# Two-layer speech encoder on one core: a correction transfer issued apart from its cast, plain down projections in every last chunk, and the opening norm sums moved into the second pair

## The chip, the core and the metric

The kernel runs on one core of one Trainium2 chip. The metric is the device time in microseconds (us); lower is better. One execution was also taken by the hardware profiler, and its profile is what this document reads. The engines run side by side, each through its own list of instructions in order: TensorE (PE, with its weight loads as PEld), VectorE (DVE), ScalarE (ACT), GpSimd (POOL) and SyncE (SP), which issues most of the DMA transfers.

## The reference

Two layers work on 512 tokens of 1024 features, all in float32. Each layer is a half-step SwiGLU feed-forward, a mixing part (attention and a convolution side by side), a second half-step SwiGLU feed-forward, and a last norm:

```python
def swiglu(x, w_gate, w_up, w_down):
    return (jax.nn.silu(x @ w_gate) * (x @ w_up)) @ w_down
...
    for l in range(DEPTH):
        x = x + 0.5 * swiglu(rms_norm(x, ffn1_norm[l]), ffn1_w_gate[l], ffn1_w_up[l], ffn1_w_down[l])
        h = rms_norm(x, mix_norm[l])
        p = h @ w_in[l]
...
        x = x + jnp.concatenate([attn, conv], axis=-1) @ w_out[l]
        x = x + 0.5 * swiglu(rms_norm(x, ffn2_norm[l]), ffn2_w_gate[l], ffn2_w_up[l], ffn2_w_down[l])
        x = rms_norm(x, post_norm[l])
```

The hidden width of each feed-forward is 2816, that is 22 blocks of 128.

## The kernel before

**Layout.** The features of x lie on the 128 partitions in eight tiles x[:, m], the 512 tokens along the free dimension. A float32 product is made of three passes: each operand is split into a rounded part (hi, type fp32r) and the rest (lo), and `mm3` (lines 152 to 154) adds weight-hi by data-hi, weight-hi by data-lo and weight-lo by data-hi into a PSUM bank. Weights are split as they arrive: a DMA into a `raw` or `fr` tile, a cast on ACT (the hi part, `wh`), and a subtraction on DVE (the lo part, `wl`). `load_w` does so for a plain product (lines 134 to 142), `split_into` for a quarter or a sum of quarters (lines 251 and 253).

**Feed-forward.** `ffn` is called four times: ffn1 and ffn2 of both layers. Its 22 hidden blocks are worked off as 11 pairs p, in four chunks of pairs, (0,1), (2,3,4), (5,6,7) and (8,9,10). In the first chunk gate and up are plain products with 512 columns (`plain`), and the result is scaled by R, the inverse root of the norm sums, only behind the product (`plain_out`, lines 300 to 305). From pair 2 on, a pair is made by seven products of quarter matrices in place of eight (`pair`, the scheme of Strassen and Winograd): the weight is loaded in quarters a11, a12, a21, a22 (line 280), four sums of them are formed on DVE, and every product has 24 matmuls of 256 columns. The data operands of these products (b11, t1, t2 and so on) are made once from x and R by the steps of the generator `operands` (lines 313 to 355), which `advance` hands out between other work. The down projection of a chunk is likewise made by seven products for each half g of the output (`down`, lines 435 to 499; 18 matmuls of 256 columns each), and each product is added to x at line 462. In the last chunk this held for ffn1 of both layers; ffn2 of both layers already had the plain form there: eight groups m of 18 matmuls of 512 columns, added to x at line 554, each followed by `done(m)`, which makes the operand of the next stage from x[:, m] (lines 165 and 166) and adds its square to the norm sums (lines 191 to 198).

**Two of the seven products** (with a12, called b21, and with a22, called t4, the fourth product) get their lo part in another way, in `summed` (lines 372 to 380): ACT writes the negated rounded quarter into a tile `ls` (line 376), and a DMA issued by POOL adds the float32 quarter from memory to it (line 377). `ls` has two buffers. Then ACT casts hi (line 379). In `down` this whole step stood at the fourth product's own place, behind the casts of the products t2, t3 and t1.

**Tiles that come round.** `fr` has four buffers, `raw` three, `wh` and `wl` four each, and PSUM gives seven banks of 512 columns. A quarter goes to an `fr` tile, except a12 and the sum s3, which go to `raw`.

**Order.** The program is written in one order and a scheduler places each engine's instructions; `tc.issue_after(order[...])` and `after(...)` hold an instruction behind a named one. From then on each engine works in order, and waits at an instruction until what it needs is there.

**The opening.** In the first ffn of layer 0 the norm sums of x stand behind pair 0. Each x[:, m] is squared on ACT; the squares were added into two sums, one by DVE and one by POOL. Sixteen tiny matmuls (8 instructions, line 205) sum them over the features, DVE scales the result (line 212), POOL takes the root (line 171), DVE lays it on a diagonal (line 220), one float32 matmul spreads it (line 224) and ACT copies it out as R (line 230). All of this stood between pair 0 and pair 1 on PE:

```python
                    if w0:
                        norm()
                        R = norm()
                    steps = operands(R)
```

Of the kernel before, what the change touches and what calls it, by code (L numbers as in the profile page):

```python
# [15 lines left out]
P = 128  # L16
# [21 lines left out]
NC = 3  # L38
# [34 lines left out]
def encoder_kernel(ctx: ExitStack, tc: tile.TileContext, xT, consts, vecs, rgain, wgu1, wd1, wdq1,  # L73
# [99 lines left out]
    class Stats:  # L173
# [5 lines left out]
        def add(self, src, scale=1.0, last=False, eng=None, apart=False, second=False):  # L179
            if second and self.tail is not None:  # L180
                sq = tmp()
                A.activation(sq, src, AF.Square, scale=scale)
                eng.tensor_tensor(self.tail, self.tail, sq, ALU.add)
                return
            if second:
                self.tail = slot()
                A.activation(self.tail, src, AF.Square, scale=scale)
                return
# [11 lines left out]
        def sums(self):  # L200
            ps = bank()
            parts = [self.acc] + ([self.tail] if self.tail is not None else [])
            for part in parts:
                for t in range(NT):
                    T.matmul(ps[:, t:t + 1], part[:, t * P:(t + 1) * P], ones[:, 0:1],
                             start=part is self.acc and (t == 0 or len(parts) == 1), stop=part is parts[-1],
                             skip_group_check=len(parts) > 1)
# [31 lines left out]
    def groups(srcs, rhs, ws=None):  # L239
# [16 lines left out]
    def ffn(l, gx, norm, wgu, wd, wdq, gain, done, w0=None, halved=KD, straight=False):  # L256
        with tc.tile_pool(name="f", bufs=4) as fpool:
            ffn_body(fpool, l, gx, norm, wgu, wd, wdq, gain, done, w0, halved, straight)

    def ffn_body(fpool, l, gx, norm, wgu, wd, wdq, gain, done, w0, halved, straight):  # L260
# [15 lines left out]
        def quarters(w, n):  # L276

            a = quarter(), late(), quarter(), quarter()
# [93 lines left out]
        def summed(w, src, n=WC):  # L372

# [3 lines left out]
            G.dma_start(out=lo[:, :n], in_=w, accum_op=ALU.add)  # L377
            hi = wpool.tile([P, WC], FR, tag="wh", name=nm("wh"))
# [3 lines left out]
        def pair(p, quartered):  # L382

            a11, a12, a21, a22, s3 = quarters(wgu[l, p], WC)
# [50 lines left out]
        def down(act, chunk):  # L435

            n = 2 * NP * P

            def finish(m):

                if chunk == NC - 1:
                    with after("added"):
                        done(m)
                        done(m + 1)

            for g in range(2):
# [3 lines left out]
                def times(o, src, name, start, q=None):  # L450
# [753 lines left out]
```

## Time and profile before

| What | Value |
|---|---|
| Median of 3 runs | 1835.67 us (1835.55 to 1839.94) |
| Profiled execution, device time | 1838.1 us |
| Its span in the profile | 1836.3 us |
| Granted TensorE clock, mean | 0.992 of full speed |
| Memory read, written | 225.30 MB, 2.10 MB |
| DMA into `ls` for a down quarter (384 KB), issue to landing, median | 6.7 us, 40 of them |
| DMA into `fr` for a gate and up quarter (512 KB), median | 4.1 us, 108 of them |

The profiled execution is 2.4 us above the median, and what lies around the span is 1838.1 - 1836.3 = 1.8 us. In the rows that follow, an instruction is given as engine, line and operation, then what it writes and what it reads; `x3` behind it counts instructions that the row takes together. In square brackets stands the time for which the engine had been idle just before, and what ended that. A row of windows gives, for one stretch of time, its length, the busy time of the engine with its number of instructions, the granted TensorE clock as a share of full speed, the busy share of the DMA engines, and what they moved.

### The profile page before, as it was taken

How to read it: one execution, taken by the hardware profiler on the slowest of the kernel's cores; microseconds unless marked ns; L12 is line 12 of the kernel's file. 1: busy time of each engine (PE TensorE's matmuls, PEld its weight loads, DVE VectorE, ACT ScalarE, POOL GpSimd, SP SyncE). 2: the span in 40 equal slices, each digit the busy share in tenths (PEclk: the TensorE clock that was granted, in tenths of full speed). 3: DMA queues.
4: the chain of work that ended last, by engine and by line, in shares of the span. 5: the costliest groups of instructions: out<-in, count | busy, mean ns of one | idle time of the engine just before them, and what ended most of it. 6: DMA issues, size and time to landing. Idle time of an engine off the chain costs nothing. (4 is left out here: it accounts for less than half of the span.)

```text
span 1836.3 us, 31207 instructions
## 1 busy us (share of the span) xinstructions
PE 1793.5 (98%) x12422; PEld 1663.6 (91%) x12422; DVE 1464.7 (80%) x2039; ACT 1108.7 (60%) x1717; POOL 435.4 (24%) x354
## 2 busy tenths in 40 slices
PE   8999999999999999999999999998999999999998
PEld 7899999888788899999889999998888788999997
DVE  6888888879965978887679878787899568878874
ACT  4565656557954565656635656565679435656564
POOL 2001000238944000000310000103579410010101
PEclk9999999999999999999999999999999999999999
DMA  4555656423303456565326474744250125465642
GB/s 163 158 138 154 156 151 157 116 76 116 69 1 110 127 155 155 149 160 139 117 68 167 112 193 113 195 116 136 75 140 21 42 85 172 119 176 135 173 116 76
DMA packets 71570, 229.42 MB, mean 125 GB/s; under 512 B 8064, under 2 KB 8448, under 8 KB 71424
## 3 DMA queue, kind: packets, MB, share of 16 engines
q1 hardware_dynamic: 54000, 169.74, 27.9%
q0 software_dynamic: 17280, 57.68, 17.8%
q8 instruction: 97, 1.59, 0.3%
q14 instruction: 49, 0.40, 0.1%
q10 hardware_dynamic: 144, 0.00, 0.0%
HBM read 225.30 MB, written 2.10 MB: 124 GB/s over the span
## 5 line engine op out<-in xcount | busy, mean ns | idle before, releaser
L152 PE MATMUL ps<-r,wh 128*128 128x256 f32 (+1 forms) x3508 | 1075.4, 309 | 6.4 <-DVE x L462 5.2
L153 PE MATMUL ps<-r,wh 128*128 128x256 f32 (+1 forms) x3508 | 1076.4, 307 | 0.0
L154 PE MATMUL ps<-r,wl 128*128 128x256 f32 (+1 forms) x2692 | 844.0, 315 | 1.4 <-DVE wl L253 0.6
L152 PEld LDWEIGHTS ps<-r,wh 128*128 128x128 f32 x3508 | 669.1, 191 | 40.6 <-issue 6.8
L153 PEld LDWEIGHTS ps<-r,wh 128*128 128x128 f32 x3508 | 670.7, 191 | 33.1 <-issue 2.7
L154 PEld LDWEIGHTS ps<-r,wl 128*128 128x128 f32 x2692 | 514.4, 191 | 34.1 <-POOL wl L142 1.3
L154 PE MATMUL ps<-r,ls 128*128 128x256 f32 x816 | 232.8, 285 | 19.7 <-DMA ls<-in_wdq 18.6
L136 ACT CAST wh<-raw 128x1024 fp32r<-128x1024 f32 (+4 forms) x132 | 118.7, 908 | 199.9 <-PE ps L153 112.3
L377 POOL DMA_DIRECT2D ls<-in_wgu x72 | 62.8, 878 | 740.8 <-ACT ls L376 695.8
L251 ACT CAST wh<-fr 128x1024 fp32r<-128x1024 f32 (+1 forms) x168 | 163.3, 972 | 97.4 <-DVE fr L392 29.4
L253 DVE TENSOR_TENSOR wl<-fr,wh 128x1024 fp32r<-128x1024 f32 (+1 forms) x168 | 189.7, 1129 | 34.6 <-ACT wh L251 34.6
L142 DVE TENSOR_TENSOR wl<-raw,wh 128x1024 fp32r<-128x1024 f32 (+4 forms) x116 | 132.1, 1146 | 70.1 <-ACT wh L136 69.5
L154 PEld LDWEIGHTS ps<-r,ls 128*128 128x128 f32 x816 | 155.5, 191 | 22.0 <-DMA ls<-in_wdq 20.7
L892 POOL TENSOR_TENSOR y<-y,pr 128x511 f32<-128x511 f32 (+14 forms) x120 | 157.5, 1313 | 54.2 <-ACT pr L888 46.9
L253 DVE TENSOR_TENSOR wl<-raw,wh 128x1024 fp32r<-128x1024 f32 (+1 forms) x112 | 125.9, 1124 | 28.4 <-ACT wh L251 27.9
L251 ACT CAST wh<-raw 128x1024 fp32r<-128x1024 f32 (+1 forms) x112 | 108.8, 972 | 37.5 <-PE ps L153 21.7
L462 DVE SCALAR_TENSOR_TENSOR x<-ps,x 128x512 f32<-128x512 f32 x140 | 96.2, 687 | 38.7 <-PE ps L154 37.9
L377 POOL DMA_DIRECT2D ls<-in_wdq x40 | 34.6, 865 | 349.7 <-ACT ls L376 315.8
L198 POOL TENSOR_TENSOR r<-r,t 128x512 f32<-128x512 f32 x45 | 78.6, 1755 | 118.7 <-ACT t L194 108.5
L376 ACT ACTIVATE ls<-fr 128x1024 fp32r<-128x1024 f32 (+1 forms) x56 | 55.1, 984 | 82.3 <-PE ps L154 55.7
L888 ACT ACTIVATE pr<-r,vec 128x511 f32<-128x511 f32 (+14 forms) x120 | 85.2, 734 | 9.7 <-POOL y L892 9.7
L884 DVE SCALAR_TENSOR_TENSOR cv<-r,vec,cv 128x511 f32<-128x511 f32 (+14 forms) x120 | 87.6, 730 | 3.4 <-ACT cv L880 2.1
(222 smaller groups left out, 2486.9 us busy)
## 6 DMA issues: line engine op xcount, KB each, us to landing
fr<-in_wgu SPq DMA_DIRECT2D x108, 512.0 KB, 4.1
ls<-in_wgu POOLq DMA_DIRECT2D x72, 512.0 KB, 5.6
raw<-in_wgu SPq DMA_DIRECT2D x66, 512.0 KB, 4.7
fr<-in_wdq SPq DMA_DIRECT2D x60, 384.0 KB, 4.6
ls<-in_wdq POOLq DMA_DIRECT2D x40, 384.0 KB, 6.7
raw<-in_wd SPq DMA_DIRECT2D x32, 256.0 KB, 2.7
raw<-in_wcv SPq DMA_DIRECT2D x16, 512.0 KB, 3.7
raw<-in_wout SPq DMA_DIRECT2D x16, 512.0 KB, 3.3
```

Of the source, the lines that this page charges most:

```text
L136: order["cast"] = A.copy(hi[:, :w], raw[:, :w]).ins
L142: (G if kind in POOLW.split() else V).tensor_tensor(lo[:, :w], raw[:, :w], hi[:, :w].bitcast(FP), ALU.subtract)
L152: T.matmul(o, lh, rh, start=first, stop=False, skip_group_check=free)
L153: T.matmul(o, lh, rl, start=False, stop=False, skip_group_check=free)
L154: order["mm"] = T.matmul(o, ll, rh, start=False, stop=last, skip_group_check=free).ins
L251: A.copy(hi[:, :w], src[:, :w])
L253: order["lo"] = V.tensor_tensor(lo[:, :w], src[:, :w], hi[:, :w].bitcast(FP), ALU.subtract).ins
L377: G.dma_start(out=lo[:, :n], in_=w, accum_op=ALU.add)
L462: return V.scalar_tensor_tensor(v, o.rearrange("p (m t) -> p m t", m=2), 0.5 * sign, v, ALU.mult, ALU.add).ins
L884: V.scalar_tensor_tensor(acc[:, s:], u[c][:, :S - s], tap(k), acc[:, s:], ALU.mult, ALU.add)
L888: A.activation(pr[:, s:], u[c][:, :S - s], AF.Copy, scale=tap(k))
L892: order["conv"] = G.tensor_tensor(acc[:, s:], acc[:, s:], pr[:, s:], ALU.add).ins
```

## The change

Three places change. First, `summed` is cut in two: `subtracted` writes the negated cast and issues the transfer, and `down` calls it for the fourth product ahead of the casts of t3, t1 and t4 itself. Second, the last chunk of every ffn takes the plain down projection; `down` loses its calls of `done`, and the weights in quarters cover two chunks, not three. Third, the opening norm sums stand within pair 1 (the second pair): the sums behind half of its first product, the spread behind its second, and all squares are added by DVE into one sum. With it come two small edits: in pair 2 the quarter a12 goes to an `fr` tile, and in the mixing part the first two groups take seven blocks of features, not six, before the rest.

```diff
-NC = 3
+NC = 2
...
-                    T.matmul(ps[:, t:t + 1], part[:, t * P:(t + 1) * P], ones[:, 0:1],
...
+                    order["sums"] = T.matmul(ps[:, t:t + 1], part[:, t * P:(t + 1) * P], ones[:, 0:1],
...
-        for ks in (range(KD - 2), range(KD - 2, KD)):
+        for ks in (range(KD - 1), range(KD - 1, KD)):
...
-            a = quarter(), late(), quarter(), quarter()
+            a = quarter(), quarter() if first else late(), quarter(), quarter()
...
-        def summed(w, src, n=WC):
-
+        def subtracted(w, src, n=WC):
 
             lo = fpool.tile([P, WC], FR, tag="ls", name=nm("ls"), bufs=2)
             A.activation(lo[:, :n], src[:, :n], AF.Copy, scale=-1.0)
             G.dma_start(out=lo[:, :n], in_=w, accum_op=ALU.add)
+            return lo
+
+        def summed(w, src, n=WC, lo=None):
+
+            lo = subtracted(w, src, n) if lo is None else lo
             hi = wpool.tile([P, WC], FR, tag="wh", name=nm("wh"))
             A.copy(hi[:, :n], src[:, :n])
             return hi, lo
...
+                lo = subtracted(wdq[l, g, chunk, 3], a22, n)
                 with after("u"):
                     times(pz, s3, "t3", True)
                 add(1, 1, pz, 1)
                 with after("v"), after("vh"):
                     times(px, a21, "t1", False)
                     order["first"] = add(1, 1, px, -1)
-                    times(pz, a22, "t4", False, 3)
+                    times(pz, a22, "t4", False, 3, lo)
...
-            last = p1 == NF // 2 and (straight or halved < KD)
+            last = p1 == NF // 2
...
-                    if w0:
-                        norm()
-                        R = norm()
-                    steps = operands(R)
-                    for o in os:
-                        act.append(plain_out(o, R))
+                    if not w0:
+                        scaled(os, R)
...
-                        plain(o, ws, range(KD))
+                        if w0 and not r:
+                            with tc.issue_after(order["mm"]):
+                                plain(o[:1], ws, KS[:KD // 2])
+                            with tc.issue_after(order["mm"]):
+                                norm()
+                            with after("sums"):
+                                plain(o[:1], ws, KS[KD // 2:])
+                                plain([None] + o[1:], ws, range(KD))
+                            with tc.issue_after(order["mm"]):
+                                R = norm()
+                            scaled(os, R)
+                        else:
+                            plain(o, ws, range(KD))
...
-            second = KS.index(m) % 2 == 1
-            st.add(x[:, m, :], eng=G if second else V, second=second)
+            st.add(x[:, m, :], eng=V)
```

`scaled(os, R)` makes the generator `operands(R)` and calls `plain_out` on pair 0's two outputs. In the changed file lines 154 and below keep their numbers; the sums stand at line 196, the spread at 215, the copy of R at 221, and lines 376, 379, 410 and 251 become 366, 374, 405 and 242.

ACT in the down projection of the first quartered chunk of layer 0, first half g, before. `e` and `t` in the second row are the silu of the pair just ended; `ls_1624` is the fourth product's negated cast, `wh_1627` its hi cast:

```order
L369 COPY e_1346<-ps_1248 128x512
L410 ACTIVATE t_1438<-e_1346 128x512
L251 CAST wh_1554<-fr_1492 128x768
L159 CAST r_1474<-t_1438 128x512
L251 CAST wh_1578<-raw_1500 128x768
L413 ACTIVATE t_1315<-ps_1248 128x256
L159 CAST r_1484<-u_1478 128x512
L159 CAST r_1488<-t_1479 128x512
L251 CAST wh_1601<-fr_1494 128x768
L376 ACTIVATE ls_1624<-fr_1495 128x768
L379 CAST wh_1627<-fr_1495 128x768
```

The same place in the changed program:

```order
L360 COPY e_1343<-ps_1245 128x512
L366 ACTIVATE ls_1575<-fr_1492 128x768
L405 ACTIVATE t_1435<-e_1343 128x512
L242 CAST wh_1551<-fr_1489 128x768
L159 CAST r_1471<-t_1435 128x512
L242 CAST wh_1578<-raw_1497 128x768
L408 ACTIVATE t_1312<-ps_1245 128x256
L159 CAST r_1481<-u_1475 128x512
L366 ACTIVATE ls_1703<-raw_1669 128x768
L159 CAST r_1485<-t_1476 128x512
L242 CAST wh_1601<-fr_1491 128x768
L374 CAST wh_1624<-fr_1492 128x768
```

The fourth product's negated cast (now `ls_1575`) has moved up by eight instructions, ahead of the silu at the head of the list, and its transfer on POOL with it.

PE in the opening, before: the end of pair 0, the sums, the spread, and the first matmuls of pair 1:

```order
L154 MATMUL ps_253<-r_158,wl_175 128x512
L205 MATMUL ps_303<-ones,r_177 128x1 x4
L205 MATMUL ps_303<-ones,r_179 128x1 x4
L224 MATMUL ps_317<-t_315,ones 128x512
L152 MATMUL ps_355<-r_105,wh_345 128x512
```

And in the changed program, first at the sums, which 12 matmuls of pair 1 now precede, then at the spread, 36 matmuls further on:

```order
L154 MATMUL ps_315<-r_132,wl_307 128x512
L196 MATMUL ps_330<-ones,r_177 128x1 x4
L152 MATMUL ps_315<-r_143,wh_311 128x512
...
L153 MATMUL ps_316<-r_159,wh_311 128x512
L154 MATMUL ps_316<-r_158,wl_313 128x512
L215 MATMUL ps_376<-t_374,ones 128x512
L152 MATMUL ps_443<-r_105,wh_433 128x512
```

So half of pair 1's 96 matmuls stand ahead of the spread now, where all of them stood behind it.

PE a little later in the changed program, in the down projection of the first chunk, where the groups 0 to 3 (`ps_531`, `ps_553`, `ps_578`, `ps_604`) go over from the third operand (`r_427`, `r_428`) to the fourth, which comes from pair 1's second product (hi `r_527`, lo `r_528`):

```order
L154 MATMUL ps_604<-r_427,wl_609 128x512
L152 MATMUL ps_531<-r_527,wh_534 128x512
L152 MATMUL ps_553<-r_527,wh_556 128x512
L152 MATMUL ps_578<-r_527,wh_581 128x512
L152 MATMUL ps_604<-r_527,wh_607 128x512
L153 MATMUL ps_531<-r_528,wh_534 128x512
```

Ahead of this place stand 36 matmuls of the four groups, and behind it 60, as before; what has moved is what stands ahead of the 36: 48 matmuls behind the spread, where there were 96.

More of the change, by code (lines that the diff above doesn't have):

```diff
@@ L177, in __init__, with add @@
             self.acc = self.tail = None
[L179 to L188, printed above, removed]
+        def add(self, src, scale=1.0, last=False, eng=None, apart=False):
             if self.acc is None:
@@ L382, in pair @@
         def pair(p, quartered):
-            a11, a12, a21, a22, s3 = quarters(wgu[l, p], WC)
+            a11, a12, a21, a22, s3 = quarters(wgu[l, p], WC, p == CHUNKS[0][1])
             bx, by, bz = bank(), bank(), bank()
@@ L448, in down, with times @@
                 px, py, pz = bank(), bank(), bank()
[L450 to L451 removed]
+                def times(o, src, name, start, q=None, lo=None):
+                    hi, lo = split_into(name, src, n) if q is None else summed(wdq[l, g, chunk, q], src, n, lo)
                     with tc.issue_after(order["pe"]):
@@ L496, in down, with scaled @@
                 add(0, 1, px, 1)
-                if chunk == NC - 1 and g:
-                    done(6)
-                    done(7)
         steps = None
+        def scaled(os, R):
+            nonlocal steps
+            steps = operands(R)
+            for o in os:
+                act.append(plain_out(o, R))
         def advance(n):
```

35 lines of the change are left out of this document (11 added, 24 removed).

## The prediction

> **What bounds the kernel now.** I read the busy shares first, then what PE waited for, then the stages around those waits.
>
> ```profile
> PE 1793.5 (98%) x12422; PEld 1663.6 (91%) x12422; DVE 1464.7 (80%) x2039; ACT 1108.7 (60%) x1717; POOL 435.4 (24%) x354
> 170.00:240.00 70.00, 70.00 (x589) 1.00 0.57 143
> 890.00:925.00 35.00, 35.00 (x156) 1.00 0.34 117
> ```
>
> PE is busy for 98% of the span, so two things can change the time: the number and width of its matmuls, and the little time in which it stands or runs at a lower clock. The two windows give its pace at full clock. In a stretch of pairs it starts 589 matmuls of 256 columns in 70 us, 0.119 us each; in a plain down projection 156 of 512 columns in 35 us, 0.224 each. A plain column is thus slightly cheaper, and I use these paces, not the duration of one matmul, since matmuls overlap. Next, the list of PE's waits:
>
> ```profile
> PE ps L154 <- DMA ls<-in_wdq: 18.6, 10, 2.1
> PE ps L152 <- DVE x L462: 5.2, 2, 2.6
> PE ps L224 <- DVE t L220: 2.9, 1, 2.9
> ...
> PE ps L154 <- DMA ls<-in_wgu: 1.1, 1, 1.1
> ...
> PE ps L154 <- DVE wl L253: 0.6, 2, 0.3
> ```
>
> Each edit aims at one of these: 18.6 us behind the fourth product's transfer, once in each of ten down projections; 5.2 us at the end of ffn1 in both layers; 2.9 us in the opening.
>
> **The fourth product's transfer.** One of the ten, in the first chunk of layer 0:
>
> ```profile
> 138.77 0.63 ACT L410 ACTIVATE t<-e 128x512 f32<-128x512 f32 x1 [2.31 <-DVE e L407]
> 144.52 0.68 DVE L160 TENSOR_TENSOR r<-u,r 128x512 fp32r<-128x512 f32 x1
> 145.90 0.84 ACT L376 ACTIVATE ls<-fr 128x768 fp32r<-128x768 f32 x1
> 147.03 0.86 POOL L377 DMA_DIRECT2D ls<-in_wdq  x1 [17.57 <-ACT ls L376]
> 153.95 0.39 PE L154 MATMUL ps<-r,ls 128*128 128x256 f32 x1 [2.08 <-DMA ls<-in_wdq]
> ```
>
> ACT made the negated tile at 145.90, POOL issued at 147.03, and the data released PE at 153.95: 6.9 us from issue to use. PE stood from 151.87. In the changed order the cast stands ahead of the silu of line 410. It still has to wait for its buffer, the second of two, which the pair's own fourth product holds; that ends just ahead of the 2.31 us wait's release, so I put the cast at 138.0 to 138.9, POOL's issue at 139.1, and the landing at 146.0. Need is at 151.87: nearly 6 us to spare, and the wait goes. ACT pays 0.84 us earlier rather than later, which moves the silu by about 0.1 us and nothing on PE: the rest of the operand for t3 is done at 144.52 + 0.68 = 145.2, and t3 starts two products of 18 x 0.119 = 2.14 us ahead of 151.6, at 147.3. POOL had been idle for 17.57 us. Next late would be b22's weights and the second half's, which in the same trace stood ready before PE came.
>
> Two of the ten waits lie in the last chunks of ffn1 and are counted below (1.54 and 1.77 us), which leaves 15.3 us. After three of the eight others PE also ran slowly:
>
> ```profile
> 153.90:158.70 4.80, 4.75 (x27) 0.64 0.93 299
> 247.90:252.70 4.80, 4.75 (x40) 1.00 0.94 299
> 1059.20:1064.00 4.80, 4.79 (x27) 0.64 0.98 306
> 1618.70:1623.50 4.80, 4.76 (x27) 0.64 0.98 311
> ```
>
> Where the granted clock behind the wait is 0.64, 27 matmuls start in 4.8 us, where it is 1.00 40 do (the one at 247.90 stands for five). The 13 missing ones are 13 x 0.119 = 1.5 us, three times 4.6 us. Term: -15.3 - 4.6 = **-19.9 us**. [...]
>
> **The last chunk of ffn1.** Both layers:
>
> ```profile
> 327.30:367.30 40.00, 35.58 (x269) 0.96 0.45 128
> 1232.60:1272.60 40.00, 35.35 (x268) 0.96 0.47 127
> 340.03 0.39 PE L154 MATMUL ps<-r,ls 128*128 128x256 f32 x1 [1.54 <-DMA ls<-in_wdq]
> 356.09 0.36 PE L152 MATMUL ps<-r,wh 128*128 128x256 f32 x1 [2.59 <-DVE x L462]
> 356.10:359.70 3.60, 3.60 (x19) 0.57 0.29 102
> 1245.59 0.39 PE L154 MATMUL ps<-r,ls 128*128 128x256 f32 x1 [1.77 <-DMA ls<-in_wdq]
> ```
>
> The windows reach from the first product of the first half to the last of the second. In them stand 2 x 7 x 18 = 252 matmuls of 256 columns, 252 x 0.119 = 30.0 us of work, and 14 matmuls of 512 columns that belong to the mixing part, 3.1 us. So the quartered form takes 40.0 - 3.1 = 36.9 us, about 7 us more than its work: the waits for `ls` and for DVE, the 0.3 us at line 253, and the slow clock (0.57) behind the 2.59 us. The plain form has 8 x 18 = 144 matmuls of 512 columns, 144 x 0.224 = 32.3 us. It asks for more PE work (+2.3) but, in ffn2 of layer 0, where it already stands with the same loads and the same `done`, the list of waits shows nothing, and the clock row of 890 to 925 says 1.00. Behind it the mixing part's first two groups have 2 x 21 matmuls, 9.4 us, to cover the last operand. Per layer 32.3 - 36.9 = -4.6; both **-9.2 us**. Bounds: with all of the waits back at the new end it would be +2.3 per layer.
>
> **Pair 2's a12 in an `fr` tile.** It frees the transfer from the `raw` tiles that the plain weights hold. In ffn2 of layer 1 this ends the 1.1 us wait on `ls<-in_wgu`: **-1.1 us**. The price is a later transfer for pair 3, whose a21 now takes the tile of pair 2's a12; that is read until the split for the last product.
>
> ```profile
> 90.35 1.23 DVE L253 TENSOR_TENSOR wl<-raw,wh 128x1024 fp32r<-128x1024 f32 x1 [1.19 <-ACT wh L251]
> 97.21 1.22 DVE L390 TENSOR_TENSOR raw<-fr,fr 128x1024 f32<-128x1024 f32 x1
> fr<-in_wgu SPq DMA_DIRECT2D x108, 512.0 KB, 4.1
> ```
>
> In layer 0's ffn1 that split ends at 91.6 and DVE first needs the new a21 at 97.2. A transfer takes 4.1 us from issue to landing, so it lands about 1 us ahead. I put this at 0, with an upper end of 1 us in each of four ffns.
>
> **The opening.** Here the sums are not simply hidden.
>
> ```profile
> 28.48 1.84 PE L205 MATMUL ps<-ones,r 128*128 128x1 f32 x16
> 33.18 2.08 PE L224 MATMUL ps<-t,ones 128*128 128x512 f32 x2 [2.87 <-DVE t L220]
> 35.29 0.59 ACT L230 COPY r<-ps 128x512 f32<-128x512 f32 x1 [5.53 <-PE ps L224]
> 35.91 0.69 DVE L300 TENSOR_TENSOR t<-ps,r 128x512 f32<-128x512 f32 x1 [2.79 <-ACT r L230]
> 33.20:39.00 5.80, 5.80 (x12) 0.50 0.06 24
> 35.90:64.50 28.60, 27.35 (x45) 0.94 0.23 74
> 58.99 0.69 DVE L304 TENSOR_TENSOR t<-ps,r 128x512 f32<-128x512 f32 x1 [1.20 <-PE ps L154]
> 63.81 0.68 DVE L160 TENSOR_TENSOR r<-t,r 128x512 fp32r<-128x512 f32 x1
> 80.55 0.28 PE L152 MATMUL ps<-r,wh 128*128 128x256 f32 x1
> ```
>
> Read at PE alone, the edit saves half of the tiny matmuls (0.9), the wait of 2.87 and the slow clock behind it (0.50 for 5.8 us), 5 to 6 us in all. But R also starts DVE, and DVE is the longer chain: from its first use of R at 35.91 to the lo part of the fourth operand at 63.81 + 0.68 = 64.5 it has 28.6 us with 27.35 busy. When does R come now? PE reaches the sums at 28.48 + 12 x 0.224 = 31.2 and the spread only 36 matmuls behind them: 31.2 + 0.9 + 8.1 = 40.2. The spread at full clock (half of 2.08) and the copy (0.59) put DVE's first use at 41.9, **6.0 us later** than before, though the root itself is done by 34. DVE's chain is shorter by two weight splits, which the order shows ahead of R now (1.2 us), and has no wait of 1.20 for PE in it: 26.2 us, so the fourth operand is whole at 68.1 and its hi part at about 66.3. PE meanwhile has 48 + 36 = 84 matmuls, 18.8 us, and is through with them at about 62 (the small waits for the first operands included). So it stands for some 4 us, and comes back at the lower clock. From 68.1 it has 56 matmuls, 12.5 us: 80.6; the rest of the slow stretch adds 1 to 2 us, and the next groups' casts, which stand on ACT behind the cast of the new a12 (its tile is freed at about 65 and lands at 69 to 70), 1 to 2 us more. Pair 2 starts at about 83.5 where it started at 80.55: **+3 us**. Bounds: -6 if DVE's chain is no bound after all, +5 if slow clock and ACT's wait add up fully.
>
> **The sum.** -19.9 - 9.2 - 1.1 + 3 = -27.2 us. Against the execution that the profile shows (1838.1) this is 1810.9; that execution was 2.4 us above the median of the runs, 1835.67, so the median to expect is 1808.5. I say **1809**.
>
> **The rivals.**
>
> (1) *The opening gains.* If the plain groups find enough work, or R comes sooner, the term goes from +3 to -5: 1801. For it speaks that DVE has had small gaps elsewhere; against it that its chain of 27.35 busy us in 28.6 follows R whatever PE does. Chance 0.12.
>
> (2) *New waits take up part of it.* With 2 us gone per down projection and one quarter bound to a later tile, something with less than 2 us to spare steps in: 1 us at pair 3 in four ffns and 0.5 in each of eight down projections, 8 us: 1817. The 0.3 us waits for line 253 show that such thin margins exist. Chance 0.15.
>
> (3) *The transfer does not come earlier*, because the cast finds its `ls` buffer held or its quarter not landed and stands until its old time: the term of -19.9 goes, 1829. Against it: the pair's fourth product ends 7 us ahead of the old cast. Chance 0.05.
>
> (4) *Slower.* The quarter a22 is asked for by these:
>
> ```profile
> 125.85 2.93 SPq L280 DMA_DIRECT2D fr<-in_wdq  x3
> fr<-in_wdq SPq DMA_DIRECT2D x60, 384.0 KB, 4.6
> ```
>
> The cast now stands ahead of the silu on ACT. If the quarter a22 lands late, ACT stands there, and the silu, the splits of u and v, and all products from t3 on are late with it. Those have 147.3 - 145.2 = 2.1 us to spare. To outweigh the gain of 27 us in eight down projections the landing has to be about 3.4 + 2.1 = 5.5 us behind 138; at 6.5 us behind it, the eight cost 8 more than they gain, 1843. Against it: the last of the three issues ends at 128.8 and 4.6 us later is 133.4, so the quarter would have to land 10 us later than it does in the median. Chance 0.03.
>
> **The numbers.** The forecast (1804 to 1814) has 0.65. The range takes in rivals 1 and 2 and the bounds of the opening: 1800 to 1818. Within 0.3% of 1835.67 (5.5 us, about what a measurement of this kernel can tell from no change) lies most of rival 3, whose 1829 is at the edge: 0.04. Faster is the rest of it with the forecast and rivals 1 and 2, 0.93; slower is rival 4, 0.03.
>
> **What would show it.** In the changed profile: no PE wait on `ls<-in_wdq`, and the negated cast ahead of the silu on ACT, about 7 us before its old place; no window at 0.64 behind the fourth product. The last chunk of ffn1: 144 matmuls of 512 columns at 1.00 without a wait, some 32 us. The opening: no wait at the spread, DVE's first use of R at about 42, then PE standing for about 4 us before the fourth operand at 66, and pair 2 starting at 83 to 84. I am wrong if pair 2 starts before 80, if PE waits for `ls` again in the down projections, or if waits of over 1 us appear at pair 3 in every ffn.

## The result and the profile after

| What | Before | After |
|---|---|---|
| Median of 4 runs each, on one chip | 1835.61 us (1835.46 to 1839.94) | 1814.38 us (1812.91 to 1815.48) |
| Ratio of the two, 95% interval | | 0.9878 (0.9861 to 0.9895) |
| Profiled execution, its span | 1838.1, 1836.3 us | 1814.81, 1813.0 us |

The time lies inside the predicted range and is 5.4 us above the predicted 1809, 5.9 above the sum before it was rounded (1808.5). 3.9 us of that are terms that came out smaller: the spans differ by 23.3 us where the terms added up to 27.2. The other 2 us are the step from the profiled execution to the median, which for before was 2.5 us and for after only 0.4. Stage by stage, cut at the same PE instructions in both traces (each mark is the start of a row; pair 2's first matmul, the norm sums and the spreads), with the terms of the prediction put where their waits lay:

| Stretch | Before | After | Difference | Predicted |
|---|---|---|---|---|
| opening, to pair 2 of layer 0 | 80.55 | 82.48 | +1.93 | +3 |
| rest of ffn1, layer 0 | 294.46 | 285.09 | -9.37 | -10.1 |
| mixing part, layer 0 | 219.53 | 219.29 | -0.24 | 0 |
| ffn2, layer 0 | 332.96 | 330.28 | -2.68 | -3.6 |
| ffn1, layer 1 | 340.17 | 331.09 | -9.08 | -9.8 |
| mixing part, layer 1 | 219.11 | 220.70 | +1.59 | 0 |
| ffn2, layer 1 | 323.21 | 317.32 | -5.89 | -6.5 |
| the end | 13.58 | 14.02 | +0.44 | 0 |

Between the ffns 12.73 us stand alike in both. First what PE waits for after the change (total, times, longest, in us), the counterpart of the list in the prediction:

```profile
PE ps L152 <- ACT r L159: 5.0, 4, 3.8
PE ps L788 <- ACT r L794: 1.9, 3, 1.1
PE ps L840 <- DVE t L829: 1.6, 2, 0.8
...
PE ps L154 <- DVE wl L142: 0.8, 3, 0.3
...
PE ps L152 <- ACT r L221: 0.7, 1, 0.7
```

No row names `ls` or the add to x any more. The longest wait is new: 3.8 us for the hi part of an operand, in the opening. Next the fourth product in the first quartered down projection, in the order of time (start, duration, engine, line):

```profile
139.98 0.85 ACT L366 ACTIVATE ls<-fr 128x768 fp32r<-128x768 f32 x1 [1.58 <-PE ps L154]
140.74 0.61 ACT L405 ACTIVATE t<-e 128x512 f32<-128x512 f32 x1
141.12 0.86 POOL L367 DMA_DIRECT2D ls<-in_wdq  x1 [9.72 <-ACT ls L366]
```

The cast stands ahead of the silu (line 405), released by PE as its buffer comes free, 1.93 us later than the prediction had it because everything starts 1.93 us later here. The windows of the same trace, for that down projection and for the plain one that now ends layer 0's ffn1 (length, busy time and matmuls, granted clock):

```profile
150.00:160.00 10.00, 9.88 (x82) 1.00 0.83 238
330.00:365.00 35.00, 35.00 (x156) 1.00 0.33 117
```

Where 27 matmuls started in 4.8 us at a clock of 0.64, 82 start in 10 us at 1.00, and the plain form runs 156 matmuls of 512 columns in 35 us, as it did in ffn2. The opening:

```profile
30.85 0.95 PE L196 MATMUL ps<-ones,r 128*128 128x1 f32 x8
39.97 1.02 PE L215 MATMUL ps<-t,ones 128*128 128x512 f32 x2
41.64 0.69 DVE L291 TENSOR_TENSOR t<-ps,r 128x512 f32<-128x512 f32 x1 [0.36 <-ACT r L221]
65.93 2.07 PE L152 MATMUL ps<-r,wh 128*128 128x512 f32 x4 [3.77 <-ACT r L159]
82.48 0.28 PE L152 MATMUL ps<-r,wh 128*128 128x256 f32 x1
```

No wait stands before the spread, but DVE uses R first at 41.64 (35.91 before), and PE stands for 3.77 us until the fourth operand is there at 65.93. Last, the one stretch that nothing in the change touches and that is slower, the end of layer 1's mixing part:

```profile
1409.95 2.08 PE L902 MATMUL ps<-t,onesm 128*128 128x512 f32 x2 [0.41 <-POOL t L900]
```

```profile
1410.00:1418.00 8.00, 8.00 (x26) 0.79 0.00 0
```

This product took 1.13 us before; the clock in the 8 us from it is 0.79.

### The profile page after: what moved, and what is told of

It is laid out like the page before. It is cut to its first block, busy times and chain, and to the rows that moved or that the text cites. A ratio compares the mean times of both kernels' runs of the same rounds, so it can differ in the third digit from the quotient of the medians.

```text
span 1813.0 us, 30598 instructions
## 1 busy us (share of the span) xinstructions
PE 1791.5 (99%) x12198; PEld 1649.3 (91%) x12198; DVE 1423.0 (78%) x1975; ACT 1089.3 (60%) x1685; POOL 422.7 (23%) x343
## 4 chain that ended last, share of the span: by engine, by line
PE 80%; DVE 9%; ACT 5%; POOL 3%; issue 2%; DMA 0%; ACTq 0%; POOLq 0%; DVEq 0%
PE ps L154 25%; PE ps L152 25%; PE ps L153 25%; POOL y L884 2%; PE ps L822 1%; ACT pr L880 1%; DVE wl L244 1%; DVE r L160 1%; DVE x L449 1%; ACT r L794 1%; PE ps L788 1%; DVE cv L876 1%; DVE wl L142 1%; DVE r L311 1%; PE ps L196 0%
## 5 line engine op out<-in xcount | busy, mean ns | idle before, releaser
L152 PE MATMUL ps<-r,wh 128*128 128x256 f32 (+1 forms) x3436 | 1062.3, 312 | 5.7 <-ACT r L159 5.0
L153 PE MATMUL ps<-r,wh 128*128 128x256 f32 (+1 forms) x3436 | 1063.9, 310 | 0.0
L152 PEld LDWEIGHTS ps<-r,wh 128*128 128x128 f32 x3436 | 652.1, 190 | 45.4 <-ACT r L159 6.7
L153 PEld LDWEIGHTS ps<-r,wh 128*128 128x128 f32 x3436 | 653.6, 190 | 36.6 <-issue 2.4
L136 ACT CAST wh<-raw 128x1024 fp32r<-128x1024 f32 (+3 forms) x148 | 132.1, 900 | 221.1 <-PE ps L153 102.8
L142 DVE TENSOR_TENSOR wl<-raw,wh 128x1024 fp32r<-128x1024 f32 (+3 forms) x132 | 146.4, 1115 | 100.1 <-ACT wh L136 93.2
L154 PE MATMUL ps<-r,ls 128*128 128x256 f32 x768 | 216.7, 282 | 0.0
L244 DVE TENSOR_TENSOR wl<-fr,wh 128x1024 fp32r<-128x1024 f32 (+1 forms) x160 | 182.3, 1139 | 39.5 <-ACT wh L242 39.5
L154 PEld LDWEIGHTS ps<-r,ls 128*128 128x128 f32 x768 | 145.2, 189 | 0.0
L244 DVE TENSOR_TENSOR wl<-raw,wh 128x1024 fp32r<-128x1024 f32 (+1 forms) x100 | 113.3, 1133 | 24.7 <-ACT wh L242 24.2
L242 ACT CAST wh<-raw 128x1024 fp32r<-128x1024 f32 (+1 forms) x100 | 97.9, 979 | 27.9 <-PE ps L153 20.0
L449 DVE SCALAR_TENSOR_TENSOR x<-ps,x 128x512 f32<-128x512 f32 x112 | 77.0, 688 | 16.5 <-PE ps L154 16.1
```

The source lines that it names most:

```text
L136: order["cast"] = A.copy(hi[:, :w], raw[:, :w]).ins
L142: (G if kind in POOLW.split() else V).tensor_tensor(lo[:, :w], raw[:, :w], hi[:, :w].bitcast(FP), ALU.subtract)
L152: T.matmul(o, lh, rh, start=first, stop=False, skip_group_check=free)
L153: T.matmul(o, lh, rl, start=False, stop=False, skip_group_check=free)
L154: order["mm"] = T.matmul(o, ll, rh, start=False, stop=last, skip_group_check=free).ins
L242: A.copy(hi[:, :w], src[:, :w])
```

## The experiments

Line numbers in each kernel's rows are its own. All medians stand together at the end of this section.

**What each edit is worth alone.** First the transfer alone, in the kernel before:

```diff
+                lo = subtracted(wdq[l, g, chunk, 3], a22, n)
                 with after("u"):
                     times(pz, s3, "t3", True)
...
-                    times(pz, a22, "t4", False, 3)
+                    times(pz, a22, "t4", False, 3, lo)
```

> The kernel before with the first edit alone: the fourth product's negated cast and its transfer stand ahead of t3, in all ten quartered down projections. My theory: the transfer was simply issued too late, so all ten waits on it go (18.6 us by the list of waits) and with them the slow clock behind three of them (about 4.5 us): 22 to 24 us less than before, about 1812 us, and no wait of PE on the fourth product's tile in the profile. Rival A, only the waits count and the clock falls anyway somewhere else: 18 to 19 us less, 1817. Rival B, the transfers now collide with others or with ACT's silu and new waits take part of it back: less than 15 us, above 1820, with new waits in the down projections.

The median is 1807.84 us, 28.3 below before and **6.5 below the whole change**. PE's waits:

```profile
PE ps L224 <- DVE t L220: 2.9, 1, 2.9
...
PE ps L152 <- DVE x L466: 0.8, 2, 0.4
```

All ten waits on `ls<-in_wdq` are gone, as expected. So is most of another one, which I had not expected: the wait at the end of ffn1 for the add to x, 2.59 us in each layer (5.2 in all, now 0.8), with its slow clock (1.00 in e1 from 312 to 363 us, where that end lies in layer 0). Then the last chunk alone, with the seven blocks ahead of the rest in the mixing part that belong to it:

```diff
-NC = 3
+NC = 2
...
-            last = p1 == NF // 2 and (straight or halved < KD)
+            last = p1 == NF // 2
```

> The kernel before with the second edit alone: plain down projection in the last chunk of ffn1 in both layers, weights in quarters for two chunks, and seven blocks ahead of the rest in the mixing part's first groups. My theory: 144 matmuls of 512 columns at 0.224 us replace 252 of 256 columns with their waits and slow clock, 8 to 9 us less in all, about 1827 us, with the other eight waits on the fourth product's tile unchanged. Rival A, the plain form only moves the waits to its end: 0 to 4 us more than before. Rival B, only the wait on the fourth product's tile counts there (1.5 and 1.8 us), so with the transfer mended this edit would be worth nothing: 3 us less at most.

1823.09 us, 13.1 below before, more than expected; of it the profile shows 11.5 us in the two ffn1 (table below). The eight other waits stayed, each a little shorter in this execution:

```profile
PE ps L154 <- DMA ls<-in_wdq: 12.4, 8, 1.6
```

Alone the two edits give 28.3 and 13.1 us, 41 together, but the whole change gives 21 (24.6 with the opening as it was, e4 below). So one must be worth less where the other is made. The second edit undone in the changed kernel (with `NC`, the calls of `done` and the six blocks of the mixing part put back as well) tells which:

```diff
-            last = p1 == NF // 2
+            last = p1 == NF // 2 and (straight or halved < KD)
```

> The changed kernel with the second edit undone: quartered down projection in the last chunk of ffn1 again (its fourth product's transfer issued early, as in the others), and six blocks ahead of the rest in the mixing part. Theory now, from the run with the transfer alone: the waits and the slow clock that made the quartered form slow there all hang on the fourth product's transfer, so with that mended the quartered form is the shorter one, 252 x 0.1197 = 30.2 us against 144 x 0.2245 = 32.3, and this kernel takes 3 to 4 us less than the changed kernel, about 1811. Rival, the prediction's own step: the plain form saves 4 us in each layer whatever else is changed, so this kernel takes 8 to 9 us more than the changed one, about 1823.

1810.78 us: 3.6 **less** than the changed kernel. The time of ffn1 from the traces, cut as in the table of the result (layer 0 from pair 2 to the next norm sums, layer 1 from the spread on):

| Kernel | Transfer early | Last chunk | Layer 0 | Layer 1 |
|---|---|---|---|---|
| before | no | quartered | 294.46 | 340.17 |
| e2 | no | plain | 288.06 | 335.09 |
| e1 | yes | quartered | 283.59 | 329.66 |
| e9 | yes | quartered | 284.07 | 329.84 |
| after | yes | plain | 285.09 | 331.09 |

Without the early transfer the plain form saves 6.4 + 5.1 us; with it, it costs 1.0 + 1.25 us against e9 (1.5 + 1.4 against e1). The other kernels with the early transfer agree: the plain form takes 285.1 to 285.6 and 331.4 to 331.6 us in e4, e5 and e8, the quartered one 283.6 and 330.0 in b1 (below). The windows of e9 show a quartered end that runs as it should, beside the one of after above: 255 matmuls in 35 us with half a microsecond of standing.

```profile
330.00:365.00 35.00, 34.48 (x255) 1.00 0.53 144
```

The spans of the two profiles differ by 2.8 us: these 2.3 us, and the slow stretch in layer 1's mixing part (1.6 us), which e9's profile doesn't have, less 1.5 us by which pair 2 came later in e9's execution (84.02).

**Why the fourth product's transfer was late.** The prediction took it as issued too late. The first run moves it less: behind t3, ahead of t1, which on ACT is one cast.

```diff
                 with after("v"), after("vh"):
+                    lo = subtracted(wdq[l, g, chunk, 3], a22, n)
                     times(px, a21, "t1", False)
```

> The kernel before with the first edit alone, but the transfer issued less early: ahead of t1's cast, which is one cast (0.74 us) ahead of the old place on ACT. Theory (the waits are the lateness of the transfer, us for us, and the clock falls only behind waits of 1.7 us and more): each of the ten waits shrinks by about 0.75 us to 0.8 to 1.2 us and no slow clock stands behind any of them, so 7.5 us of waiting and 4 to 5 us of slow clock go: 1824 to 1827. Rival A, the clock falls behind any wait in some of the cases: 1828 to 1830. Rival B, the wait is for something that comes with t1 or t4 and not for the transfer: as before, 1836.

1814.93 us: all the waits on `ls<-in_wdq` are gone, not 7.5 us of them, and the theory "us for us" fell; eight short waits of up to 1.3 us for the add to x stand in their place (6.2 us). In before the next transfer on POOL was issued 1.47 us behind this one, and here 2.20 us. So the next theory was that the two share POOL's queue; the run takes them apart without moving the first:

```diff
-                times(py, a12, "b21", True, 1)
+                with tc.issue_after(order["apart"]) if g else nullcontext():
+                    times(py, a12, "b21", True, 1)
...
                     times(px, a12, "b22", False)
+                    order["apart"] = order["hi"]
```

(`order["hi"]` is the last hi cast of `split_into`.)

> The kernel before, with nothing moved for the fourth product: its negated cast and transfer stay at their old place. Instead the negated cast of the second half's b21, which stood right behind it on ACT (POOL issued the two transfers 1.47 us apart), is held behind two later casts, so that its transfer is issued about 4 to 5 us behind the first. Theory now, from the run with the transfer 0.74 us earlier: the two transfers of 384 KB share the queue's bandwidth while both are in flight, so the first needs 6.9 us from issue to use; alone it would need about 4.9, land at about 151.9 in the first down projection, just where PE needs it, and the waits of 1.5 to 2.1 us go nearly whole, with their slow clock: 15 to 22 us less than before, 1814 to 1821. Rival: the transfer is simply issued too late (6.9 us is what it takes there); then the ten waits stay as they are and the time is 1836.

1836.97 us, as before: the second transfer now came 5.4 us behind (146.16 and 151.53), and the first took as long as ever. The theory fell. What had stayed in place was SP. Its two transfers for the second half start when the fourth product's hi cast has ended, which frees the quarter's tile; in before that cast ends at 147.46 (start 146.64, 0.82 us), and SP follows:

```profile
147.49 1.09 SPq L280 DMA_DIRECT2D fr<-in_wdq  x2
```

```profile
DMA to landing us min/median/max: 6.9/6.9/6.9
```

The second fence is the tile view of `ls` at POOL's issue of 147.03: 6.9 us to land. SP follows it by 0.46 us. In e11 (the timeline of POOL and SP):

```profile
146.16 0.86 POOL L377 DMA_DIRECT2D ls<-in_wdq  x1 [17.57 <-ACT ls L376]
146.62 1.08 SPq L280 DMA_DIRECT2D fr<-in_wdq  x2
```

Again 0.46 us. In e10 it is 1.19 us (the window of this row ends before SP's second issue):

```profile
146.59 0.86 POOL L376 DMA_DIRECT2D ls<-in_wdq  x1 [16.84 <-ACT ls L375]
147.78 0.33 SPq L280 DMA_DIRECT2D fr<-in_wdq  x1
```

The last run therefore leaves both POOL transfers where they are and holds SP back, by writing the hi cast twice:

```diff
-            A.copy(hi[:, :n], src[:, :n])
+            for _ in range(2 if twice else 1):
+                A.copy(hi[:, :n], src[:, :n])
```

> The kernel before, with the fourth product's negated cast, its transfer and the next one on POOL left where they are. Only its hi cast on ACT is written twice (the same values), the second time behind the next negated cast. The hi cast frees the quarter's tile, and SP issues two transfers of the second half as soon as it ends, 0.46 us behind POOL's issue in the kernel before (147.49 and 147.03 in the first down projection); with the second cast they come about 1.9 us behind it. Theory now: the fourth product's transfer takes 6.9 us there and not 4.7 because SP's two transfers start with it, as in the run with POOL's two transfers held apart (6.8 us still, SP 0.46 us behind) and unlike the run with the transfer 0.74 us earlier (4.7 us, SP 1.2 us behind). So it now takes about 4.8 us, and the ten waits on it shrink from 18.6 us in all to under 6, with no slow clock behind them: 12 to 20 us less than before, 1816 to 1824, unless SP's later transfers are themselves waited for. Rival: the transfer takes 6.5 to 6.9 us at that place in any case; the waits stay at 17 to 19 us and the time is 1836.

1824.86 us, 12.8 below before and just above the 1816 to 1824 expected, with the fourth product's transfer left in its place. SP came 1.21 us behind POOL, less than the 1.9 expected, and it was enough. POOL and SP, and the landing:

```profile
147.25 0.86 POOL L377 DMA_DIRECT2D ls<-in_wdq  x1 [17.57 <-ACT ls L376]
148.46 1.05 SPq L280 DMA_DIRECT2D fr<-in_wdq  x2
```

```profile
DMA to landing us min/median/max: 4.9/4.9/4.9
```

| Kernel | POOL's issue | SP behind it | Landing of the fourth product's transfer | In all ten first halves |
|---|---|---|---|---|
| before | 147.03 | 0.46 | 6.9 | 6.3 to 6.9 |
| e11 | 146.16 | 0.46 | 6.8 | 6.4 to 6.8 |
| e12 | 147.25 | 1.21 | 4.9 | 4.6 to 4.9 |
| e10 | 146.59 | 1.19 | 4.7 | 4.4 to 4.8 |
| e1 | 138.02 | 8.9 | 4.6 | 4.5 to 4.9 |

The last column takes the first half of every one of the ten quartered down projections, where the ten waits of before stand. In e12's list of waits 0.5 us are left on `ls<-in_wdq` of 18.6, and it shows what the later SP transfers cost in turn, splits that come late by up to 1 us:

```profile
PE ps L154 <- DVE wl L253: 4.3, 10, 1.0
PE ps L152 <- DVE x L463: 2.7, 3, 1.1
...
PE ps L154 <- DMA ls<-in_wdq: 0.5, 2, 0.2
```

So 2.0 of the 6.9 us come from SP's transfers starting beside this one, and 0.75 us of room, with POOL earlier or SP later, ends that. The packets in the traces show how. These rows give the packets, megabytes and share of the DMA engines' time by queue in the 1.8 us that begin 1.42 us behind POOL's issue, first in before (148.45 to 150.25), then in e12 (148.67 to 150.47). Each has one queue alone, SP's (q1) in before and POOL's (q0) in e12:

```profile
q1 hardware_dynamic: 77, 0.24, 84.6%
```

```profile
q0 software_dynamic: 67, 0.21, 93.3%
```

In all ten first halves of before and e11 SP's packets begin 1.4 us behind POOL's issue, and POOL's own only 3.3 to 3.9 us behind it, when SP's first transfer (384 KB) is nearly through. In e1, e10 and e12 POOL's begin at about 1.6 us, and in e10 and e12 SP's wait until 3.6 to 4.0. In these kernels the transfer whose packets came first went ahead. SP's came about 1 us behind their issue and POOL's 1.6 us, so with 0.46 us between the issues SP's passed. In before the two queues then shared the DMA engines for about 1 us (47.8% for SP's and 45.8% for POOL's from 150.4 to 150.9, 29.5% and 81.0% in the next half microsecond), and from 151.4 to 152.4 POOL's had them nearly alone (0.20 MB, SP's 0.01). The shortest landing that these kernels show for the fourth product's transfer is 4.4 us.

**The opening.** The move alone, in the kernel before (the third edit of the change, its diff as above):

> The kernel before with the third edit alone: the opening norm sums behind half of pair 1's first product, the spread behind its second, all squares added by DVE. My theory: R comes 6 us later and DVE's chain from R to the fourth operand (about 26 us) bounds the opening, so pair 2 starts 2 to 3 us later than before (82.5 to 83.5 us) and the time is 2 to 3 us more. Rival A, read at PE alone: the wait at the spread, the slow clock and half of the tiny matmuls go, pair 2 starts at about 75 us and the time is 5 us less. Rival B: the loss in the changed kernel comes from something else that stands there (the fr tile in pair 2), and this edit alone costs nothing.

1837.71 us, ratio 1.0003 (0.9994 to 1.0013): at most 2.4 us slower and not told from no change. Pair 2 starts at 81.54, 1.0 us later than in before and not the 2 to 3 expected. Its profile has the same wait as the changed kernel and the spread's wait gone:

```profile
PE ps L152 <- ACT r L159: 5.0, 4, 3.8
```

And the changed kernel with the opening as it was:

```diff
-                    if not w0:
-                        scaled(os, R)
+                    if w0:
+                        norm()
+                        R = norm()
+                    scaled(os, R)
```

> The changed kernel with the opening put back as it was (sums and spread between pair 0 and pair 1, squares added by DVE and POOL into two sums). My theory: 2 us less than the changed kernel, pair 2 starting at about 80.5 us where it started at 82.48. Rival A, the move saves time at PE: 5 us more than the changed kernel. Rival B, the later stages take up the difference: the same time as the changed kernel.

1811.58 us, 2.8 less, with pair 2 at 79.72. That start varies from one execution to the next: with the old opening it lies between 79.38 and 81.02 (seven profiles, mean 80.3), with the moved one between 81.54 and 84.02 (after, e3, e8 and e9, mean 82.5). So the move costs about 2 us. That R's place sets it, and not the move as such, is told by the spread put 24 matmuls earlier:

```diff
-                                plain([None] + o[1:], ws, range(KD))
                             with tc.issue_after(order["mm"]):
                                 R = norm()
+                            with after("spread"):
+                                plain([None] + o[1:], ws, range(KD))
```

> The changed kernel with the spread 24 matmuls earlier: behind pair 1's first product, not behind its second. Theory: the later start of pair 2 comes from R's place in PE's list alone, because DVE's chain of about 26 us from R to the fourth operand is the longer one; R comes at about 36.3 us (41.6 in the changed kernel), the wait of 3.8 us for the fourth operand goes, and pair 2 starts at 76 to 78 us (82.5): 5 to 6 us less than the changed kernel, 1809. Rival: DVE's chain only stretches (it takes in other weight splits first), and PE waits for the same operand at the same time: the same time as the changed kernel.

1809.36 us, 5.0 less than the changed kernel:

```profile
36.59 0.69 DVE L291 TENSOR_TENSOR t<-ps,r 128x512 f32<-128x512 f32 x1 [2.37 <-ACT r L221]
61.92 0.50 PE L152 MATMUL ps<-r,wh 128*128 128x512 f32 x1 [1.49 <-ACT r L159]
77.71 0.28 PE L152 MATMUL ps<-r,wh 128*128 128x256 f32 x1
```

DVE has R at 36.59, 5.05 us earlier, the fourth operand is there 4.01 us earlier, and pair 2 starts 4.77 us earlier. The last one changes only the order of DVE's work behind R:

```diff
-                        advance(8)
-                        act.append(plain_out(o, R))
+                        if w0:
+                            act.append(plain_out(o, R))
+                            advance(8)
```

> The changed kernel with the order of DVE's work behind R changed alone: in pair 1 of the opening the output of each product is scaled before the next eight operand steps, so the fourth operand has less ahead of it on DVE; R stays where it is. Theory (DVE's chain sets the wait): the wait of 3.8 us for the fourth operand becomes shorter by 1 to 3 us and pair 2 starts 1 to 3 us earlier, if the operand steps that are put off do not come late at pair 2. Rival: ACT or the weight splits set the wait; pair 2 starts at 82.5 as before.

Pair 2 starts 4.4 us earlier, more than the 1 to 3 us expected, and the time is 1815.98, 1.6 us more than the changed kernel. The waits have only moved into pair 2:

```profile
78.09 0.28 PE L152 MATMUL ps<-r,wh 128*128 128x256 f32 x1
...
82.07 0.39 PE L154 MATMUL ps<-r,ls 128*128 128x256 f32 x1 [0.70 <-DMA ls<-in_wgu]
87.01 0.38 PE L152 MATMUL ps<-r,wh 128*128 128x256 f32 x1 [2.08 <-ACT wh L242]
88.27 0.39 PE L154 MATMUL ps<-r,wl 128*128 128x256 f32 x1 [0.76 <-DVE wl L244]
```

At the next norm sums (367.50, after: 367.57) nothing of the 4.4 us is left. The work behind R that was put off came back as waits on ACT and DVE; of the two runs, only the one with an earlier R kept what it gained.

**Pair 2's a12** back in a `raw` tile, in the changed kernel:

```diff
-            a11, a12, a21, a22, s3 = quarters(wgu[l, p], WC, p == CHUNKS[0][1])
+            a11, a12, a21, a22, s3 = quarters(wgu[l, p], WC)
```

> The changed kernel with pair 2's a12 in a raw tile again. Theory: the wait of about 1 us on the transfer into that quarter comes back in ffn2 of layer 1, and the short wait for a plain weight's lo part in the first chunk of ffn2 (about 0.6 us in each layer with what it slows) goes; together within 1 us of the changed kernel. Rival A: those 0.6 us are not from this edit; then only the 1 us comes back, 1815.5. Rival B: the later transfer for pair 3 costs about 1 us in each ffn, and this kernel takes 3 us less than the changed one.

1813.44 us, 0.9 less than the changed kernel, inside both intervals. Two rows of its waits:

```profile
PE ps L154 <- DVE wl L142: 0.3, 1, 0.3
PE ps L154 <- DMA ls<-in_wgu: 0.2, 1, 0.2
```

The wait of about 1 us doesn't come back (0.2), and of the plain weights' waits 0.5 us go (0.8 in the changed kernel). The edit is worth nothing that can be told.

**The parts that gain, together**: the early transfer, the last chunk left quartered, a12 left in `raw`, the opening with the early spread.

> The parts that the runs have shown to gain, together: the kernel before with the early transfer (first edit) in all ten quartered down projections, the last chunk of ffn1 left quartered, pair 2's a12 left in a raw tile, and the opening moved with the spread behind pair 1's first product. Theory: the transfer alone gave 1807.8; pair 2 starts 1 to 2 us earlier than in that run (77.7 us in the run with the early spread, 79.4 to 80.5 with the opening as before): 1805 to 1807, under the changed kernel by 8 to 9 us. Rival: the early spread and the quartered last chunk disturb each other's transfers and weight splits, 1808 or more.

1804.75 us (1803.29 to 1806.33), **9.6 below the changed kernel** and 32.7 below before. What its PE still waits for, the longest rows:

```profile
PE ps L816 <- ACT r L822: 2.1, 4, 1.1
PE ps L152 <- ACT r L159: 1.8, 3, 1.5
PE ps L868 <- DVE t L857: 1.6, 2, 0.8
```

| Kernel | Median us | Before beside it | Ratio, 95% interval |
|---|---|---|---|
| e1 transfer alone | 1807.84 | 1836.14 | 0.9836 (0.9819 to 0.9853) |
| e2 last chunk alone | 1823.09 | 1836.14 | 0.9920 (0.9902 to 0.9937) |
| e3 opening alone | 1837.71 | 1836.14 | 1.0003 (0.9994 to 1.0013) |
| e4 after, old opening | 1811.58 | 1836.14 | 0.9859 (0.9840 to 0.9878) |
| e5 after, earlier spread | 1809.36 | 1835.97 | 0.9860 (0.9840 to 0.9880) |
| e6 after, DVE reordered | 1815.98 | 1835.97 | 0.9890 (0.9874 to 0.9907) |
| e8 after, a12 in raw | 1813.44 | 1835.97 | 0.9876 (0.9861 to 0.9891) |
| e9 after, quartered last chunk | 1810.78 | 1835.97 | 0.9862 (0.9847 to 0.9876) |
| e10 transfer less early | 1814.93 | 1837.48 | 0.9894 (0.9877 to 0.9910) |
| e11 POOL's transfers apart | 1836.97 | 1836.55 | 1.0000 (0.9991 to 1.0010) |
| e12 SP's transfers later | 1824.86 | 1837.69 | 0.9937 (0.9922 to 0.9952) |
| b1 the gaining parts | 1804.75 | 1837.48 | 0.9825 (0.9812 to 0.9838) |

Each kernel was timed beside before, whose own median moved by 1.7 us from group to group (1835.97 to 1837.69), so two kernels compare best by their ratios: by these e5 lies 3.3 us and e9 2.9 us below the changed kernel, not 5.0 and 3.6. Their intervals overlap its 0.9861 to 0.9895, as do those of e4, e6 and e8, and b1's overlaps e1's; there it is the stretches of the traces that carry the text. Only e1 and b1 lie clear below the changed kernel.

## Why the prediction was right, and where it was not

**The fourth product (-19.9): right, and the margin for another reason.** The four ffn stretches gave 0.6 to 0.9 us less each than predicted, in all -27.0 for -30.0 with the last chunk. Cast and issue came where they were put (139.98 and 141.12, that is 138.0 and 139.2 without the later opening). The step that failed is "the landing at 146.0": it took the old 6.9 us along to a new place. There the transfer takes 4.5 us, with no transfer of SP's starting beside it (the next is issued 8.9 us behind it, at 149.99), so the margin is over 8 us and not "nearly 6". It changed nothing in the sum, but it is the cause of the wait, shown by e10, e11 and e12: the transfer wasn't so much issued late as held up for 2 us by SP's, which was issued 0.46 us behind it.

**The last chunk of ffn1 (-9.2): the size of the stage about right, its cause wrong.** The prediction counted 7 us of waits and slow clock as the price of the quartered form, and let the plain form save them. But they hung on the transfer, which the first edit mends in that chunk too: the two waits on `ls` (1.54 and 1.77), by the list of e1 also the 2.59 us at line 462, and the slow clock behind it. Given the first edit, the second saves nothing and costs what the bare work says, 32.3 - 30.2 = 2.1 us per layer by the two paces; measured were 1.0 to 1.5. The prediction had "+2.3 per layer" only as a bound for waits at the new end. With the two edits priced on the same trace one after the other, the sum came out near enough only because the first edit gained what the second was credited with; so far that is luck, and the advice would have been wrong. Why the wait at line 462 ended with the transfer stays open. In before, DVE does two steps for the next operand (3.45 us) ahead of that add, and in e1 the order has them apart, but that alone doesn't explain it: in layer 0, e12 has the two together (3.47 us) and waits 1.11 us there, and e10 has them apart and waits 1.26.

**The opening (+3, measured +1.9): right in mechanism and in its points.** First use of R 41.64 for 41.9, standing of 3.77 us for "some 4", until 65.93 for 66. Pair 2 came at 82.48, not 83.5: the term "the next groups' casts, 1 to 2 us" didn't come. From 65.93 the 60 matmuls took 16.6 us where 13.4 is full pace (60 x 0.224), and the slow clock (0.50 from 65.9 to 71.7, 14 matmuls in 5.8 us where 26 would fit) covers most of the difference. The rival of -5, read at PE alone, is refuted by e3 and e4, since in both pairs the moved opening starts pair 2 later.

**Pair 2's a12 (-1.1): wrong.** The wait went, but e8 shows it down to 0.2 us without the edit as well, and in e3, which doesn't have the edit either, no such wait stands; in e2 and e11 it is 1.2 and 1.8 us. It varies with the execution.

**Not foreseen: +1.6 in layer 1's mixing part.** The same product at a lower clock stands in the profiles of e2 and e6 too, and not in the other eleven. All three have the plain last chunk, but so have e4, e5 and e8, which don't show it. I take it for a matter of the single execution; what sets it off stays open.

**New waits (rival 2, 8 us)** came to under 1 us: 0.5 us more for plain weights' lo parts.

## What to carry to other kernels

Two edits that cure the same wait must not be priced one after the other on the trace of before: ask of the second what is left once the first is made, and time each alone and each undone. A transfer's time belongs to its moment (here 6.9 us at the old place and 4.5 at the new): before moving a late DMA, look at what other queues issue within a microsecond of it, whose packets come first, and what freed their tiles. Moving work off the engine that waits can still lose (about 2 us in this opening) if the moved instruction is also the start of a longer chain elsewhere; move its place in the list by halves rather than all the way.

## What the runs showed of the hardware

Behind some of PE's waits of about 2 us the granted clock fell, and behind others it did not. In the four kernels whose PE waited for the fourth product's transfer (before, e2, e3, e11) there are 38 such waits: none of the 17 of at most 1.70 us was followed by slow work, and 7 of the 21 of 1.72 to 2.08 us were (27 matmuls started in the next 4.8 us, not 39 or 40, at a mean granted clock of 0.64 each time). All six waits of 2.58 to 2.59 us at the end of ffn1 were (20 to 28 matmuls, at 0.50 to 0.70). In all the clock fell behind 13 of these 44. What makes waits of like length go both ways no run shows: in before the clock was 0.64 in the 4.8 us behind a wait of 1.73 us (at 1059.21) and 1.00 behind one of 2.01 us (at 1153.27).
